# Hybrid mLSTM and DeltaNet layer step: the end of the kernel reordered, and the DeltaNet level product on 128x128 tiles

## The chip, the cores and the metric

One Trainium2 chip, one of its cores, one launch. The metric is the time of an execution on the device in microseconds (us); the number that counts is the median of the runs.

## The reference

One decoder layer for a prompt of 512 tokens and 8 sample sequences of 4 tokens (32 sample tokens), width 2048, all in f32. The layer is: a modulation of the input by `silu(c) @ w_ada`, one input projection, four mLSTM heads and eight gated DeltaNet heads, an output projection with a layer norm, a SwiGLU feed-forward block of inner width 5632 with a second layer norm, and the updated states. Two places matter here. The DeltaNet step solves, for each head and chunk, a unit lower triangular system:

```
A = bet[..., :, None] * jnp.einsum('bhld,bhsd->bhls', kh, kh) * decay * strict
sol = lax.linalg.triangular_solve(eye + A, rhs, left_side=True, lower=True, unit_diagonal=True)
```

and the layer ends with the down projection and a layer norm over the 2048 columns of each token, `(xf - mu) * lax.rsqrt(var + LN_EPS) * g + b`:

```
ffn = (jax.nn.silu(gate) * up) @ w_down
x = layer_norm(DEEPNORM_ALPHA * x + (1 + gt2) * ffn, ln2_g, ln2_b)
```

## The kernel before, in words

The kernel is one program for all engines. Activations stand transposed in SBUF, features on the 128 partitions and 544 columns of tokens (512 of the prompt, then 32 of the samples). A weight product is done in three passes of a rounded f32 format: `split` (L147) makes a high part of a weight on ScalarE (a copy, L97) and the remainder on VectorE (a subtraction, L100); the activations were split in the same way. `split_w` (L151) does it for eight blocks of 128x128 at a time, with two buffers for each part. Weights come in on SP's queue into three buffers (`raw_tile`). Helpers record every ScalarE activation at L97, every `tensor_tensor` at L100 (VectorE, or GpSimd where the call names it) and every `scalar_tensor_tensor` at L103.

The order on each engine is not the order of the text. A planner puts the instructions into each engine's stream before the launch, by the order of the text as priority and by its own estimate of when operands and buffers are there. Each engine then works through its stream in order, waiting on semaphores.

**DeltaNet.** `gdn_solve` (L595) prepares one head: four chunks of 128 tokens on the free dimension. It builds the inverse `U` of the triangular matrix by doubling: seven levels n, block size b = 2^n. Level 0 is a mask and transposes. In each of the six others (L646 to L679) GpSimd masks the coupling blocks into `Al` (128 x 4 chunks x 64 columns), VectorE copies the even blocks of `U` into `Ue`, TensorE transposes `Ue` (L666, two transposes for the four chunks), and multiplies `Al` of each chunk with the odd blocks of `U` (L669): four f32 products with 64 stationary and 64 moving columns, of which two chunks go to the upper and two to the lower 64 partitions of the PSUM tile `ps`. ScalarE copies the result into the block diagonal tile `P1` in two copies (L97), VectorE copies the transposes into `Tm`; a second product (L677, two f32 products of 128x128 with 128 columns) and a subtraction from the odd blocks of `U` end the level. `gdn_chain` (L682) then runs the recurrence over chunks. `weave` (L189, L1201) interleaves the solve of head hd+1 and the chain of head hd with the generator `fill` of dense projection products (L160), which keep TensorE supplied.

**The end.** `down` (L1502) is the down projection, in three rounds over the 44 blocks of the inner width (0 to 14, 14 to 28, 28 to 44). The last round has m = 0 to 11 over all 544 columns; m = 12 to 15 are done in two halves of the columns: first 0 to 256 (token tiles 0 and 1), then 256 to 544 (token tiles 2, 3 and the samples). A block m of a half is two loads of eight 128x128 weight blocks, 48 products (L1520) and an update of `z[m]` on VectorE (L103), with three small operations for the sample columns when the half has them. The half blocks and the turned tiles share a pool of three PSUM buffers (L1500).

`turned(j, ts)` (L1563) turns four feature blocks of each token tile with four transposes (L1569) into one PSUM tile, takes its statistics (L1570) and copies it to SBUF on ScalarE. The samples are the fifth token tile, with 32 of 128 partitions in use. `norm(t0, t1)` (L1573) aggregates the statistics, makes the reciprocal root by Ln and Exp on ScalarE for all its tiles together, and then goes through the tiles in four pieces of 512 columns: for the first three pieces Identity with scale and bias on ScalarE, the product with the gain on VectorE, the sum with the shift on GpSimd; for the fourth two fused operations on VectorE. Two stores of 1024 columns for each tile (L1595).

The order of the end (L1599 to L1611): m = 0 to 11, where after each four of them five tiles are turned; the first half of m = 12 to 15; of the second half m = 12; turning of tiles 0 and 1; m = 13; then m = 14 and 15 together with `norm(0, 2)`; turning of tiles 2, 3 and the samples; `norm(2, 5)`.

## Time and profile before

| | us |
|---|---|
| median of three runs (lowest to highest) | 3022.82 (3014.93 to 3023.85) |
| the profiled execution | 3026.12 |
| its span, first to last instruction | 3024.3 |
| TensorE busy in the span | 2934.8 |
| VectorE busy | 1710.0 |
| ScalarE busy | 1118.2 |
| GpSimd busy | 311.4 |

Engines in rows: PE is TensorE's matmul, PEld its weight load, DVE is VectorE, ACT ScalarE, POOL GpSimd, SP the engine that issues DMAs; a q behind the name marks the issuing side. A transpose stands as MATMUL too. Matmuls are pipelined: a record's duration is its way through the array, and what TensorE spends on it is the distance from its start to the next start. A row of the timeline merges instructions of one kind that follow each other (x8), with the start of the first, the time to the end of the last, and in brackets the idle time of the engine ahead of it and what ended that. Rows by window give for each stretch its length, busy time and number of instructions of each engine, the granted clock as a share of full speed, the busy share of the DMA engines and GB/s.

### The profile page before, as it was taken

How to read it: one execution, taken by the hardware profiler on the slowest of the kernel's cores; microseconds unless marked ns; L12 is line 12 of the kernel's file. 1: busy time of each engine (PE TensorE's matmuls, PEld its weight loads, DVE VectorE, ACT ScalarE, POOL GpSimd, SP SyncE). 2: the span in 40 equal slices, each digit the busy share in tenths (PEclk: the TensorE clock that was granted, in tenths of full speed). 3: DMA queues.
4: the chain of work that ended last, by engine and by line, in shares of the span. 5: the costliest groups of instructions: out<-in, count | busy, mean ns of one | idle time of the engine just before them, and what ended most of it. 6: DMA issues, size and time to landing. Idle time of an engine off the chain costs nothing.

```text
span 3024.3 us, 55954 instructions
## 1 busy us (share of the span) xinstructions
PE 2934.8 (97%) x22642; PEld 2733.7 (90%) x22642; DVE 1710.0 (57%) x3000; ACT 1118.2 (37%) x2053; POOL 311.4 (10%) x475
## 2 busy tenths in 40 slices
PE   8999999999999999999899999999999999999995
PEld 5788788888888989899799999999999999999995
DVE  2443433254555666655787777777777753333336
ACT  3333223234444444432354444444444432222224
POOL 0000101010121222210220000000000020000003
PEclk9999999999999999999899999999999999999998
DMA  8856666665445332443333433334343464433224
GB/s 271 283 161 171 200 189 192 196 200 165 148 124 157 90 89 68 132 131 102 121 111 114 118 113 109 113 113 120 106 116 113 117 214 112 138 105 110 84 78 135
DMA packets 567222, 418.02 MB, mean 138 GB/s; under 512 B 26956, under 2 KB 500132, under 8 KB 566964
## 3 DMA queue, kind: packets, MB, share of 16 engines
q1 hardware_dynamic: 554644, 378.74, 42.6%
q0 software_dynamic: 12320, 35.71, 3.4%
q8 instruction: 178, 2.92, 0.4%
q14 instruction: 80, 0.66, 0.1%
HBM read 374.21 MB, written 40.15 MB: 137 GB/s over the span
## 4 chain that ended last, share of the span: by engine, by line
PE 66%; issue 5%; DMA 2%; DVE 2%; ACT 2%; POOL 1%; SPq 0%; POOLq 0%; ACTq 0%; DVEq 0%
PE P L1380 29%; PE d L1520 16%; PE d L160 12%; PE P L1445 2%; PE m L1520 1%; PE a L232 1%; PE m L677 1%; DMA S<-in_state_gdn_S_dram 1%; PE m L669 1%; DMA raw<-in_w_out_dram 0%; ACT jk L97 0%; DVE lo L100 0%; ACT hi L97 0%; PE m L666 0%; PE m L807 0%
## 5 line engine op out<-in xcount | busy, mean ns | idle before, releaser
L97 ACT ACTIVATE hi<-raw 128x1024 fp32r<-128x1024 f32 (+3 forms) x384 | 369.0, 961 | 784.0 <-PE d L160 307.4
L100 DVE TENSOR_TENSOR lo<-raw,hi 128x1024 fp32r<-128x1024 f32 (+3 forms) x384 | 427.6, 1114 | 305.3 <-ACT hi L97 294.5
L160 PE MATMUL d<-hhi,hi 128*128 128x272 f32 x2048 | 461.2, 306 | 1.2 <-ACT hi L97 1.2
L160 PE MATMUL d<-hhi,lo 128*128 128x272 f32 x2048 | 429.4, 290 | 0.0
L160 PE MATMUL d<-hlo,hi 128*128 128x272 f32 x2048 | 427.7, 289 | 0.0
L160 PEld LDWEIGHTS d<-hhi,hi 128*128 128x128 f32 x2048 | 321.3, 189 | 86.3 <-issue 39.3
L160 PEld LDWEIGHTS d<-hlo,hi 128*128 128x128 f32 x2048 | 322.3, 189 | 3.2 <-issue 2.3
L160 PEld LDWEIGHTS d<-hhi,lo 128*128 128x128 f32 x2048 | 322.8, 189 | 0.9 <-issue 0.3
L100 DVE TENSOR_TENSOR lo<-lw,hi 128x1024 fp32r<-128x1024 f32 x84 | 103.0, 1226 | 181.7 <-ACT hi L97 181.7
L97 ACT ACTIVATE hi<-lw 128x1024 fp32r<-128x1024 f32 x84 | 89.2, 1062 | 193.6 <-PE P L1380 191.4
L1520 PE MATMUL d<-alo,hi 128*128 128x272 f32 x896 | 150.8, 290 | 4.1 <-DVE s L100 4.1
L103 DVE SCALAR_TENSOR_TENSOR s<-d,adaT,s 128x512 f32<-128x512 f32 x76 | 57.0, 750 | 171.2 <-PE d L1520 119.9
L1520 PE MATMUL d<-ahi,hi 128*128 128x272 f32 x896 | 149.3, 288 | 0.0
L1380 PE MATMUL P<-ahi,s 128*128 128x272 f32 x1008 | 140.5, 288 | 0.0
L1380 PE MATMUL P<-alo,s 128*128 128x272 f32 x1008 | 140.5, 288 | 0.0
L97 ACT ACTIVATE s<-lw 128x512 fp32r<-128x512 f32 x168 | 106.2, 632 | 84.8 <-PE P L1380 54.5
L1406 POOL DMA_DIRECT2D hid<-s x88 | 47.2, 543 | 828.1 <-DVE s L100 786.1
L1380 PEld LDWEIGHTS P<-ahi,s 128*128 128x128 f32 x1008 | 132.3, 188 | 0.0
L1380 PEld LDWEIGHTS P<-alo,s 128*128 128x128 f32 x1008 | 132.1, 188 | 0.1
L1520 PEld LDWEIGHTS d<-alo,hi 128*128 128x128 f32 x896 | 128.2, 190 | 4.3 <-issue 4.3
L1380 PE MATMUL P<-ahi,hi 128*128 128x272 f32 x672 | 130.0, 288 | 0.0
L1380 PE MATMUL P<-alo,hi 128*128 128x272 f32 x672 | 129.4, 287 | 0.0
(715 smaller groups left out, 6561.9 us busy)
## 6 DMA issues: line engine op xcount, KB each, us to landing
araw<-in_w_ada_dram SPq DMA_DIRECT2D x288, 256.0 KB, 3.9
raw<-in_w_in_dram SPq DMA_DIRECT2D x104, 512.0 KB, 5.5
raw<-in_w_gu_dram SPq DMA_DIRECT2D x168, 256.0 KB, 4.1
s<-in_w_gu_dram SPq DMA_DIRECT2D x168, 256.0 KB, 3.2
raw<-in_w_down_dram SPq DMA_DIRECT2D x72, 512.0 KB, 4.0
araw<-in_w_ada_dram SPq DMA_DIRECT2D x48, 512.0 KB, 6.0
raw<-in_w_out_dram SPq DMA_DIRECT2D x32, 512.0 KB, 4.8
raw<-in_w_down_dram SPq DMA_DIRECT2D x32, 384.0 KB, 3.5
```

The costliest lines, as they stand in the source:

```text
L97: A.activation(out, in_, func, **kw)
L100: eng.tensor_tensor(out, in0, in1, op)
L103: V.scalar_tensor_tensor(out, in0, scalar, in1, op0, op1)
L160: PE.matmul(ps[:, 240 + HALF * h:240 + HALF * (h + 1)], w_, a_[:, HALF * h:HALF * (h + 1)], start=f, stop=l)
L232: PE.matmul(ps[32 * g:32 * g + 32, :128 * nt], cT[:, q + g, :], rw[g // n][:, g % n, :], start=(q == 0), stop=end)
L669: PE.matmul(ps[r:r + 64, 64 * (c // 2):64 * (c // 2) + 64].rearrange("p (n b) -> p n b", b=b), Al[:, c, :], part(U, 1)[:, c], start=True, ...
L677: PE.matmul(ps[:, 256 + 128 * c:384 + 128 * c], ch(Tm, c), P1[:, c, :], start=True, stop=True)
L1380: PE.matmul(ps[n], w_[:, kk, :], block(b, x, k), start=f_, stop=l_)
L1406: G.dma_start(hid[2 * c + m][:, HALF * h:HALF * h + HALF], ut[m ^ h][:, HALF * m:HALF * m + HALF])
L1445: PE.matmul(acc_n[t][h], wn[m // 4 * 4, t // 2][:, m % 4, 128 * (t % 2):128 * (t % 2) + 128], z[m][:, HALF * h:HALF * h + HALF], start=(m ...
L1520: PE.matmul(ps[:, b - c0:e - c0], w_[:, kk, :], H[k][x][:, b:e], start=f, stop=l)
```

## The change

**DeltaNet (`gdn_solve`).** `Al` becomes one flat tile of 4 x 64 columns. Two chunks at a time are the stationary side of one product, 128 columns, and the odd blocks of the same two chunks its 128 moving columns. The result is 128x128 for a pair of chunks; the two 64x64 blocks on its diagonal are the wanted products, and the two copies into `P1` pick those. Two f32 products take the place of four.

**The end.** The samples leave `turned`: the new `norm_s` brings their 32 tokens x 2048 columns onto 128 partitions (four groups of 32 partitions, one for each 512 columns) with 16 products against the identity, takes statistics for each partition, combines the four groups with two products against `same4` (0.25 where two partitions belong to the same token), and normalises all in one 128x512 piece with gains and shifts that eight more loads put on the same partitions. The halves of m = 12 to 15 change places: columns 256 to 544 come first, 0 to 256 last, so that token tiles 0 and 1 are the last ones. Each block of a half has a yield between its two weight loads. The fourth turned part of tiles 0 and 1 stays in PSUM (`held`) and is normalised from there. The reciprocal root is Sqrt on ScalarE and a reciprocal on VectorE, with one Sqrt at the start of the stretch instead of the named table. All sums with the shift are on VectorE; the fourth piece is handled like the others. Stores of the last two tiles are 512 columns each.

```diff
@@ -645,7 +645,8 @@
         idb = ident.unsqueeze(1).to_broadcast([128, 4, 128])
         for n in range(7):
             b = 1 << n
-            Al = T(mp, [128, 4, 128], "Al", bufs=1)[:, :, :128 if n == 0 else 64]
+            al_ = T(mp, [128, 512], "Al", bufs=1)[:, :512 if n == 0 else 256]
+            Al = al_.rearrange("p (c t) -> p c t", c=4)
             part = lambda t, e: t.rearrange("p c (n e b) -> p c n e b", e=2, b=b)[:, :, :, e, :]
             if n == 0:
                 tt(Al, Am, lev[:, 0:1, :].to_broadcast([128, 4, 128]), ALU.mult, G)
@@ -664,18 +665,19 @@
             ps, pt = pst(), pst()
             for c in range(2):
                 PE.transpose(ch(pt, c), Ue[:, 2 * c:2 * c + 2, :].rearrange("p c t -> p (c t)"), ident)
-            for c in range(4):
-                r = 64 * (c % 2)
-                PE.matmul(ps[r:r + 64, 64 * (c // 2):64 * (c // 2) + 64].rearrange("p (n b) -> p n b", b=b),
-                          Al[:, c, :], part(U, 1)[:, c], start=True, stop=True)
-            for r in (0, 64):
-                act(P1[r:r + 64, :, r:r + 64], ps[r:r + 64, 0:128].rearrange("p (c s) -> p c s", c=2), AF.Copy)
+            uo = U.rearrange("p c (n e b) -> p (c n) e b", e=2, b=b)[:, :, 1, :]
+            for c in range(2):
+                PE.matmul(ch(ps, c).rearrange("p (n b) -> p n b", b=b), ch(al_, c),
+                          uo[:, 128 // b * c:128 // b * (c + 1)], start=True, stop=True)
+            for e in range(2):
+                r = 64 * e
+                act(P1[r:r + 64, :, r:r + 64],
+                    ps[r:r + 64, 0:256].rearrange("p (c e s) -> p c e s", c=2, e=2)[:, :, e, :], AF.Copy)
             Tm = T(mp, [128, 256], "Tm", bufs=1)
             V.tensor_copy(Tm, pt[:, 0:256])
             yield
             for c in range(2):
                 PE.matmul(ps[:, 256 + 128 * c:384 + 128 * c], ch(Tm, c), P1[:, c, :], start=True, stop=True)
-            uo = U.rearrange("p c (n e b) -> p (c n) e b", e=2, b=b)[:, :, 1, :]
             tt(uo, uo, ps[:, 256:].rearrange("p (n b) -> p n b", b=b), ALU.subtract)
             yield
 
@@ -1512,6 +1515,8 @@
             ahead.clear()
             for i, rw in enumerate(loaded):
                 n = min(8, k1 - k0 - 8 * i)
+                if i and c1 - c0 < NT:
+                    yield
                 h3, l3 = split_w(rw, n)
                 for k in range(k0 + 8 * i, k0 + 8 * i + n):
                     kk = k - k0 - 8 * i
@@ -1549,66 +1554,111 @@
 
 
     free = [t[:, :1024] for h in range(2) for t in cx_tiles(h, F32)]
-    yn, grow = [free[2 * t:2 * t + 2] for t in range(5)], free[10:12]
+    yn, grow, cx_last = [free[2 * t:2 * t + 2] for t in range(4)], free[8:10], free[10:12]
     brow = [T(lx, [128, 2 * NT], "lw%d" % i)[:, :1024] for i in range(2)]
     for row, n in ((grow, "ln2_g"), (brow, "ln2_b")):
         for i in range(2):
             SP.dma_start(row[i], a[n][1024 * i:1024 * i + 1024].unsqueeze(0).to_broadcast([128, 1024]))
-    bst = T(lx, [128, 5, 4, 6], "bst")
-    mv = T(lx, [128, 5, 4], "mv")
-    V.memset(mv, 1.0)
-    A.preload_act_table_set("natural_log_exp_and_others")
-    rows = [128] * 4 + [NS]
+    bst = T(lx, [128, 4, 4, 6], "bst")
+    mv = T(lx, [128, 4, 4], "mv")
+    act(mv[:, 0, 0:1], eps_l, AF.Sqrt)
+
+    def turn_tile(j, t):
+
+        ps = pst()
+        for i in range(4):
+            PE.transpose(ps[:, 128 * i:128 * i + 128], z[4 * j + i][:, 128 * t:128 * t + 128], ident)
+        V.bn_stats(bst[:, t, j, :], ps)
+        return ps
+
+    def y_of(t, j):
+        return yn[t][j // 2][:, 512 * (j % 2):512 * (j % 2) + 512]
+
+    def row_of(x, j):
+        return x[j // 2][:, 512 * (j % 2):512 * (j % 2) + 512]
 
     def turned(j, ts):
-
         for t in ts:
-            n, c = rows[t], 512 * (j % 2)
-            ps = pst()
-            for i in range(4):
-                PE.transpose(ps[:n, 128 * i:128 * i + 128], z[4 * j + i][:, 128 * t:128 * t + n], ident)
-            V.bn_stats(bst[:n, t, j, :], ps[:n])
-            act(yn[t][j // 2][:n, c:c + 512], ps[:n], AF.Copy)
-
-    def norm(t0, t1):
-        for t in range(t0, t1):
-            V.bn_aggr(mv[:rows[t], t, 0:2], bst[:rows[t], t, :, :])
-        act(mv[:, t0:t1, 2], mv[:, t0:t1, 1], AF.Ln, bias=eps_l)
-        act(mv[:, t0:t1, 2], mv[:, t0:t1, 2], AF.Exp, scale=-0.5)
-        stt(mv[:, t0:t1, 3], mv[:, t0:t1, 0], -1.0, mv[:, t0:t1, 2], ALU.mult, ALU.mult)
-        for t in range(t0, t1):
-            n = rows[t]
-            mean, rstd, off = (mv[:n, t, i:i + 1] for i in (0, 2, 3))
+            act(y_of(t, j), turn_tile(j, t), AF.Copy)
+
+    def scales(m):
+
+        mean, var, rstd, off = (m[..., i:i + 1] for i in range(4))
+        act(rstd, var, AF.Sqrt, bias=eps_l)
+        V.reciprocal(rstd, rstd)
+        stt(off, mean, -1.0, rstd, ALU.mult, ALU.mult)
+
+    def norm(ts, held=None):
+
+        for t in ts:
+            V.bn_aggr(mv[:, t, 0:2], bst[:, t, :, :])
+        scales(mv[:, ts[0]:ts[-1] + 1])
+        for t in ts:
+            for j in (3, 0, 1, 2) if held else range(4):
+                y = y_of(t, j)
+                act(y, held[t] if held and j == 3 else y, AF.Identity, scale=mv[:, t, 2:3], bias=mv[:, t, 3:4])
+                tt(y, y, row_of(grow, j), ALU.mult)
+                tt(y, y, row_of(brow, j), ALU.add)
+                if held:
+                    SP.dma_start(y_p[0, 128 * t:128 * t + 128, 512 * j:512 * j + 512], y)
+                elif j % 2:
+                    SP.dma_start(y_p[0, 128 * t:128 * t + 128, 512 * j - 512:512 * j + 512], yn[t][j // 2])
+                yield
+
+    def norm_s():
+
+        ps = pst()
+        for i in range(4):
             for j in range(4):
-                c = slice(512 * (j % 2), 512 * (j % 2) + 512)
-                y, g_, b_ = (x[j // 2][:n, c] for x in (yn[t], grow, brow))
-                if j < 3:
-                    act(y, y, AF.Identity, scale=rstd, bias=off)
-                    tt(y, y, g_, ALU.mult)
-                    tt(y, y, b_, ALU.add, G)
-                else:
-                    stt(y, y, mean, g_, ALU.subtract, ALU.mult)
-                    stt(y, y, rstd, b_, ALU.mult, ALU.add)
-                if j % 2:
-                    c = slice(1024 * (j // 2), 1024 * (j // 2) + 1024)
-                    dst = y_p[0, 128 * t:128 * t + 128, c] if t < 4 else y_s2[:, c]
-                    SP.dma_start(dst, yn[t][j // 2][:n])
-            yield
+                PE.matmul(ps[32 * j:32 * j + 32, 128 * i:128 * i + 128], z[4 * j + i][:, SEQ:], ident, start=True,
+                          stop=True)
+        V.bn_stats(sst, ps)
+        act(ys, ps, AF.Copy)
+        V.bn_aggr(ms[:, 0:2], sst.unsqueeze(1))
+        yield
+
+        ps = pst()
+        PE.matmul(ps[:, 0:1], same4, ms[:, 0:1], start=True, stop=True)
+        tt(ms[:, 2:3], ms[:, 0:1], ps[:, 0:1], ALU.subtract)
+        V.tensor_copy(ms[:, 0:1], ps[:, 0:1])
+        stt(ms[:, 1:2], ms[:, 2:3], ms[:, 2:3], ms[:, 1:2], ALU.mult, ALU.add)
+        yield
+        PE.matmul(ps[:, 1:2], same4, ms[:, 1:2], start=True, stop=True)
+        V.tensor_copy(ms[:, 1:2], ps[:, 1:2])
+        scales(ms)
+        act(ys, ys, AF.Identity, scale=ms[:, 2:3], bias=ms[:, 3:4])
+        tt(ys, ys, gbs[:, 0], ALU.mult)
+        tt(ys, ys, gbs[:, 1], ALU.add)
+        for j in range(4):
+            SP.dma_start(y_s2[:, 512 * j:512 * j + 512], ys[32 * j:32 * j + 32])
+        yield
 
     y_s2 = y_s.rearrange("b t c -> (b t) c")
+
+    gbs = cx_last[0][:, :1024].rearrange("p (x c) -> p x c", x=2)
+    ys = cx_last[1][:, :512]
+    ms, sst = cx_last[1][:, 512:516], cx_last[1][:, 516:522]
+    same4 = cx_last[1][:, 528:656]
+    for x, n in enumerate(("ln2_g", "ln2_b")):
+        for j in range(4):
+            SP.dma_start(gbs[32 * j:32 * j + 32, x], a[n][512 * j:512 * j + 512].unsqueeze(0).to_broadcast([32, 512]))
+    V.tensor_reduce(same4[:, 0:32], ident.rearrange("p (j t) -> p t j", j=4), mybir.AxisListType.X, ALU.add)
+    V.tensor_scalar(same4[:, 0:32], same4[:, 0:32], 0.25, None, ALU.mult)
+    V.tensor_copy(same4[:, 32:128].rearrange("p (j t) -> p j t", j=3),
+                  same4[:, 0:32].unsqueeze(1).to_broadcast([128, 3, 32]))
     part = down(range(12), 28, 44)
     for j in range(3):
         for _ in range(4):
             next(part)
-        turned(j, range(5))
-    drain(down(range(12, 16), 28, 44, 0, 256))
-    part = down(range(12, 16), 28, 44, 256, NT)
+        turned(j, range(4))
+    drain(down(range(12, 16), 28, 44, 256, NT))
+    part = down(range(12, 16), 28, 44, 0, 256)
     next(part)
-    turned(3, range(2))
     next(part)
-    run_gens(part, norm(0, 2))
-    turned(3, range(2, 5))
-    drain(norm(2, 5))
+    turned(3, (2, 3))
+    run_gens(part, chain(norm_s(), norm((2, 3))))
+    held = {t: turn_tile(3, t) for t in (0, 1)}
+    drain(norm((0, 1), held))
     op_stack.close()
     lx_stack.close()
     pj_stack.close()
```

## Rows read from the trace of the kernel before

**Rows 1.** The page: TensorE's busy time, share of the span and instructions, and its busy tenths in 40 slices of the span.

```profile
PE 2934.8 (97%) x22642; PEld 2733.7 (90%) x22642; DVE 1710.0 (57%) x3000; ACT 1118.2 (37%) x2053; POOL 311.4 (10%) x475
PE   8999999999999999999899999999999999999995
```

**Rows 2.** Busy time by window, the DeltaNet stage.

```profile
775.00:1300.00 525.00, 508.71 (x4138) 461.99 (x4138) 320.65 (x740) 235.18 (x621) 119.50 (x183) 1.00 0.39 112
```

**Rows 3.** The instructions of L669: durations in ns (least, median, most), first and last start in us, form.

```profile
L669 PE MATMUL m<-s,Al x192: 218/222/275, 778.5 to 1214.4; 128*64 128x64 f32 x192
...
L669 PE MATMUL m<-U,Al x192: 218/222/273, 833.9 to 1296.6; 128*64 128x64 f32 x192
```

**Rows 4.** Timeline from the last weight product to the last store, rows of PE, DVE, ACT and SP.

```profile
2991.01 0.82 PE L1569 MATMUL m<-cst,s 128*128 128x128 f32 x6
...
2992.13 0.47 DVE L103 SCALAR_TENSOR_TENSOR s<-m,adaT,s 128x256 f32<-128x256 f32 x1
...
2993.30 0.68 DVE L1570 BATCH_NORM_STATS2 bst<-m 128x6 f32<-128x512 f32 x1
...
2995.73 0.48 DVE L1575 BATCH_NORM_AGGREGATE mv<-bst 128x2 f32<-128x24 f32 x3
...
2996.44 1.28 ACT L97 ACT_TABLE_LOAD   x1
2997.73 0.30 ACT L97 ACTIVATE mv<-mv,cst 128x3 f32<-128x3 f32 x1
2998.05 1.28 ACT L97 ACT_TABLE_LOAD   x1
...
2999.58 0.17 DVE L103 SCALAR_TENSOR_TENSOR mv<-mv 128x3 f32<-128x3 f32 x1 [2.10 <-ACT mv L97]
2999.79 1.52 ACT L97 ACTIVATE c4a<-c4a,mv 128x512 f32<-128x512 f32 x2 [0.23 <-DVE mv L103]
...
3017.37 0.32 SPq L1595 DMA_DIRECT2D out_dram<-c3b  x1
```

**Rows 5.** Timeline of the half-width part, rows of DVE and PE.

```profile
2953.50 0.48 DVE L103 SCALAR_TENSOR_TENSOR s<-m,adaT,s 128x256 f32<-128x256 f32 x1 [0.63 <-PE m L1520]
...
2959.15 0.48 DVE L103 SCALAR_TENSOR_TENSOR s<-m,adaT,s 128x256 f32<-128x256 f32 x1 [0.63 <-PE m L1520]
...
2970.97 1.03 PE L1569 MATMUL m<-cst,s 128*128 128x128 f32 x8
2971.17 0.48 DVE L103 SCALAR_TENSOR_TENSOR s<-m,adaT,s 128x256 f32<-128x256 f32 x1 [0.99 <-PE m L1520]
...
2979.78 1.22 DVE L100 TENSOR_TENSOR lo<-raw,hi 128x1024 fp32r<-128x1024 f32 x1
...
2981.01 1.28 DVE L100 TENSOR_TENSOR c0a<-c0a,c4b 128x512 f32<-128x512 f32 x2
...
2990.39 1.82 DVE L103 SCALAR_TENSOR_TENSOR c3a<-c3a,mv,lw 128x512 f32<-128x512 f32 x1
```

**Rows 6.** Timeline of PE in the DeltaNet stage: one level, and two products of the chain.

```profile
996.31 0.38 PE L666 MATMUL m<-cst,Ue 128*128 128x128 f32 x2
996.62 0.45 PE L669 MATMUL m<-U,Al 128*64 128x64 f32 x8
997.00 0.52 PE L160 MATMUL d<-hhi,hi 128*128 128x272 f32 x2
997.36 0.42 PE L160 MATMUL d<-hlo,hi 128*128 128x272 f32 x2
...
999.37 0.61 PE L677 MATMUL m<-P,Tm 128*128 128x128 f32 x4
999.73 0.50 PE L160 MATMUL d<-hhi,hi 128*128 128x272 f32 x2
1000.07 0.41 PE L160 MATMUL d<-hlo,hi 128*128 128x272 f32 x2
...
1093.22 0.38 PE L689 MATMUL m<-S,s 128*128 128x128 f32 x2
1093.44 0.39 PE L690 MATMUL m<-S,s 128*128 128x128 f32 x2
```

**Rows 7.** Timeline of PE in the full-width part: one turning of the samples.

```profile
2838.57 0.60 PE L1569 MATMUL m<-cst,s 128*32 128x128 f32 x4
2838.92 0.50 PE L1520 MATMUL d<-alo,hi 128*128 128x272 f32 x2
```

**Rows 8.** Timeline at the step from the full-width to the half-width part, rows of ACT and PE.

```profile
2938.40 0.60 ACT L97 ACTIVATE c1a<-m 128x512 f32<-128x512 f32 x1 [2.00 <-DVE bst L1570]
2939.05 1.31 PE L1569 MATMUL m<-cst,s 128*128 128x128 f32 x8 [1.93 <-ACT c1a L97]
```

**Rows 9.** Busy time by window in the half-width part (PE, PEld, DVE, ACT, POOL, then the granted clock).

```profile
2940.40:2943.80 3.40, 3.40 (x16) 3.40 (x17) 0.69 (x2) 1.18 (x2) 0.00 (x0) 0.51 0.15 45
...
2971.00:2991.00 20.00, 20.00 (x153) 19.91 (x152) 18.59 (x32) 13.68 (x17) 9.22 (x4) 1.00 0.35 106
```

**Rows 10.** Timeline of PE in the DeltaNet stage: a product that waits for another engine.

```profile
1091.22 1.09 PE L807 MATMUL m<-S,kq 128*64 128x128 f32 x8 [1.15 <-POOL kq L100]
```

**Rows 11.** Timeline of SP's queue at the step from the second to the third round of the down projection.

```profile
2784.00 0.57 SPq L1556 DMA_DIRECT2D c4b<-in_ln_g_dram  x1
...
2789.38 5.14 SPq L144 DMA_DIRECT2D raw<-in_w_down_dram  x2
```

More of the change, by code (lines that the diff above doesn't have):

```diff
@@ L2 @@
 from contextlib import ExitStack
-from itertools import islice, zip_longest
+from itertools import chain, islice, zip_longest
 import numpy as np
```

## The prediction

> **What bounds the kernel now.** I read the page first: the busy shares and the slices. TensorE is busy 97% of the span, nine tenths or more in nearly every slice, and only the last slice falls to five tenths [rows 1]. So what is taken off TensorE's stream counts nearly in full until its last weight product, and behind that product something else sets the end. Each part of the change has its own stretch, and is priced there.
>
> In the DeltaNet stage (775 to 1300 us) TensorE is busy 508.7 of 525 us, VectorE 320.7, ScalarE 235.2, GpSimd 119.5 [rows 2]: TensorE is the bound and the others only time its rare stops. The level product stands in the trace as 2 x 192 = 384 records on 128*64 tiles [rows 3], that is 8 heads x 6 levels x 4 chunks x 2 records for an f32 product: 48 groups of eight.
>
> The end I read in the timeline, backwards. The last weight product is over at 2991.01, where the turning of the last tiles begins; the last store is issued at 3017.37 [rows 4]; the span ends at 3024.3. From the last product to the end are 33.3 us in which TensorE hardly works. In them VectorE and GpSimd work side by side in SBUF and slow each other: an operation on 128x512 takes 0.64 us where VectorE is alone (two in 1.28) and 1.82 beside GpSimd [rows 5]. Two table loads of 1.28 us stand between the statistics and the first normalised value [rows 4].
>
> **The change part by part.**
>
> **DeltaNet product: -6.2 us.** Before, two transposes start at 996.31, the eight half-width records at 996.62, the next dense pair at 997.00 and the pair behind it at 997.36 [rows 6]: 1.05 us. In this the two transposes hold 0.31 us, where two full records followed by full ones hold 0.22 (1093.22 to 1093.44); entering the half-width shape costs time outside the group. After, the group is four full 128x128 f32 records, the very shape of the second product of the same level: 999.37 to 999.73, then a dense pair to 1000.07, together 0.70 [rows 6]. With 0.22 for the transposes that is 0.92, so 0.13 less, 48 times: -6.2. Bounds: if only the group itself counts, 0.38 against 0.36, it is -1.0. If the four records take 0.11 each like those at 1093, 0.44 against 0.38 and no gain outside, it is +2.9. I take -6.2, since every shape in the sum has a row and the stage is TensorE's. The two evictions, the transposed copy and GpSimd's mask keep count and size: nothing. The first eviction now waits for the last record rather than an earlier one; the dense products between the two halves of a level hide that.
>
> The Trainium skill, page "TensorEngine Tiling (Array Packing)", section "Theoretical Speedup", promises up to twice the speed to a product whose stationary side has at most 64 columns; by that the merged product would cost up to twice the 0.38 us, which is a rival below. The same page's "Key Properties" says that a change of tiling mode drains the engine, and the 0.31 against 0.22 of rows 6 agrees with it.
>
> **Turning of the samples: 0.** Three turnings of the 32-token tile leave TensorE's stream in the full-width part; one holds 0.35 us (2838.57 to 2838.92) [rows 7], -1.0 in all. norm_s puts 16 f32 products (32 records) on 128*32 tiles instead, four column groups at once: as an estimate eight steps at the 0.11 of a 128-column record plus entry and exit, +1.1.
>
> **The step into the half-width part: -0.6.** Five turned tiles pass three PSUM buffers there, and TensorE waits 1.93 us at 2939.05 for the first copy [rows 8]. With four tiles, one copy (0.6) less has to be over before the next product. The clock's fall to 0.51 right behind [rows 9] I leave as it is, since a wait of the same kind stays.
>
> **Waits that are added: +1.0.** Three products of norm_s hang on small VectorE and ScalarE work. TensorE takes its stream in order, so the weight products behind them wait too, and behind those the copies that free the weight tiles. The nearest rows are 1.93 us (a turning that waits for a copy) and 1.15 us (a product that waits for GpSimd's mask) [rows 8, 10]. Two waits at half the smaller: +1.0; bounds 0 and +4. The eight added loads of gains pass SP's queue ahead of weight loads: at 0.57 us of issue each 4.6 us, where the next weight load came 5.4 us after the first gain load [rows 11]; weights are three tiles ahead, so nothing, and without that cover up to 4.6 once.
>
> **The end: -8.0.** Let S be the turning of tiles 2 and 3. From S to the last product TensorE has three output blocks of 256 columns at 5.65 us (from update to update, 2953.50 to 2959.15), 1.0 for the turning [rows 5] and 1.1 for the samples: 19.1 us. In this time VectorE is given five weight remainders at 1.22 (6.1), three updates at 0.48 (1.4), three statistics at 0.68 (2.0) [rows 4, 5], their aggregates (0.6), nine small steps of the samples at 0.17 (1.5), two rows of the samples (1.3) and eight pieces of 128x512 at 1.28 for tiles 2 and 3 (10.2): 23.1 us. In the same stretch VectorE is now busy 18.6 of 20 us [rows 9], so 1.4 idle; 17.7 get done and 5.4 are left over at the last product. What follows, by rows of the present end [rows 4]: 0.2 to the update (as 2970.97 to 2971.17), 1.2 from the update to the first statistics, 1.3 for two of them, 0.4 aggregates, 0.35 root, 0.2 reciprocal (no row has it at this size; between 0.17, a small step, and 0.68, a full-width one, nearer the first), 0.2 offset, 0.8 for the first Identity: 4.7 us, of which 2.3 leave VectorE free for the leftover. Then sixteen operations at 0.64 (10.2), the other 3.1 of the leftover, and from the last store's issue to the end 7.0 as now plus 0.3, the last store being larger: 25.3 against 33.3. Gone are the sample tile's four pieces, both table loads (2.6) and every 1.82. Bounds: no leftover at all, -11.1; all of it behind and another 0.7 lost, -5.
>
> That the root keeps one table for good rests on the rows so far only by likeness: Identity follows the second load without another [rows 4]. The Trainium skill, page "ScalarE: Activation LUTs", section "Table sets: the hidden batching unit", says that one set holds both Ln and Exp, so that one load serves both; by that only 1.3 us would go here. The trace shows two loads in a row, and the rows decide.
>
> **Sum.** -6.2 + 0 - 0.6 + 1.0 - 8.0 = -13.8 us. The profiled execution took 3026.12 us, 1.8 over its span and 3.3 over the median of the runs; from the median, 3022.8 - 13.8 = 3009.0.
>
> **Rivals.**
> 1. *The merged product gives nothing*, because TensorE's gain turns into waits for the level's copies. For it: ScalarE's evictions and VectorE's subtraction time every level. Against it: TensorE stands still for only 16 of 525 us [rows 2]. Time: 3009.0 + 6.2 = about 3015. Chance 0.13.
> 2. *VectorE becomes the bound of the end*: the order on each engine is planned beforehand, the leftover stays in front of the last tiles, and the weights' remainders come late too. For it: VectorE is full already [rows 9] and takes over GpSimd's additions. The end then gains 4 rather than 8 and the waits cost 2 more: about 3015. Chance 0.15.
> 3. *Slower: the samples' products stop TensorE long enough for its clock to fall.* At 2939.05 it had stood 1.93 us, and soon after it ran at 0.51, the lower of its levels (1.2 instead of 2.4 GHz) [rows 8, 9]. If each of the three products waits for VectorE's leftover (some 3 us each, +9) and the 17 us of blocks behind them run at half clock (+17), the sum is +12: about 3035. It decides once the waits pass some 3 us each with the clock down. Against it: in that stretch TensorE is now busy 20 of 20 us beside a full VectorE. Chance 0.07.
> 4. *Slower: half-width tiles are worth their factor of two.* Then the merged product costs 0.38 more, 48 times, +18 instead of -6: about 3033. Against it: the same shape at 0.36 [rows 6]. Chance 0.03. This is the rule of the tiling page.
>
> **How the numbers follow.** Forecast 0.62, rivals 0.13, 0.15, 0.07 and 0.03. 0.3%, about what a measurement can tell from no change, is 9.1 us, so the line lies at 3013.7. The forecast's own bounds are 3005 (no wait, no leftover: -6.2 - 0.6 - 11.1) and 3020 (-1.0 - 0.6 + 4 - 5); the runs shown lie 9 us apart, so the lower end goes to 3001, and rivals 1 and 2 are inside. Range 3001 to 3019. Rivals 1 and 2 lie near the line, mostly above it: faster 0.66, same 0.24, slower 0.10.
>
> **What would show it.** Right: the level product as four records on 128*128 tiles (192 in all), about 0.92 us from the first transpose to the second dense pair; no GpSimd work behind the last product; VectorE's pieces at 0.64; no table load at the end; some 25 us from the last product to the end. Wrong: over 4 us of idle time before the samples' products, a granted clock under 1 between S and the last product, more than four leftover pieces behind the last product, or waits in the DeltaNet stage that grow by the 6 us saved.

## The result and the profile after

| | before | after |
|---|---|---|
| median of six runs, taken side by side | 3021.55 us | 3004.06 us |
| lowest to highest | 3014.93 to 3024.44 | 3003.07 to 3006.33 |
| ratio, 95% interval | | 0.9949 [0.9940, 0.9959] |
| the profiled execution, its span | 3026.12, 3024.3 | 3004.57, 3002.8 |

By the ratio the change takes off 15.4 us (12 to 18); 13.8 were forecast. The profiled spans lie 21.6 us apart, and stretches that the change does not touch make up the difference: the DeltaNet stage begins at 760.8 before and 757.8 after, and over all thirteen traces of this study that start varies from 754.1 to 760.8. Below, stretches are compared, not spans, and products are counted from their starts. Five of them carry the result (from the timelines); they add up to some 15.5 us:

| us | before | after |
|---|---|---|
| first solve to last inverse level of the DeltaNet stage | 537.3 | 533.6 |
| first weight product of the down projection to its last full-width one | 490.1 | 488.4 |
| last full-width product to last product | 55.6 | 58.1 |
| last product to the end of the span | 33.5 | 19.3 |
| TensorE's wait at the layer norm behind the output projection | 7.0 | 8.6 |

The page of the kernel after, parts 1 and 2, beside [rows 1]: TensorE's last slice rises from five tenths to seven, GpSimd loses 15 operations.

```profile
PE 2927.0 (97%) x22470; PEld 2738.0 (91%) x22470; DVE 1702.9 (57%) x3016; ACT 1114.4 (37%) x2050; POOL 282.7 (9%) x460
PE   8999999999999999999899999999999999999997
```

The instructions of the merged product, L670, of the kernel after (columns as in [rows 3]): 192 records on 128*128 where there were 384 on 128*64.

```profile
L670 PE MATMUL m<-s,Al x96: 273/275/280, 774.9 to 1206.6; 128*128 128x128 f32 x96
...
L670 PE MATMUL m<-U,Al x96: 273/275/347, 830.6 to 1290.0; 128*128 128x128 f32 x96
```

One level in TensorE's timeline, after, beside [rows 6]: transposes at 991.33, product at 991.55 (0.22 later, not 0.31), second dense pair at 992.25. The level takes 0.92 us, the number of the forecast.

```profile
991.33 0.38 PE L667 MATMUL m<-cst,Ue 128*128 128x128 f32 x2
991.55 0.61 PE L670 MATMUL m<-U,Al 128*128 128x128 f32 x4
991.91 0.49 PE L160 MATMUL d<-hhi,hi 128*128 128x272 f32 x2
992.25 0.41 PE L160 MATMUL d<-hlo,hi 128*128 128x272 f32 x2
```

The end in the timeline, after, beside [rows 4]. The last weight product starts at 2983.50. VectorE still owes four pieces of token tile 3 (c1b; the last tiles, 0 and 1, stand in c0a to c3a), but they mostly fill the pauses of the chain update, statistics, aggregates, root, reciprocal. The first piece of the last two tiles starts at 2989.24, sixteen operations follow at 0.6 each, and the last store goes out at 2999.23, 3.6 us before the end. There is no table load in this stretch, and no GpSimd.

```profile
2983.82 0.48 DVE L103 SCALAR_TENSOR_TENSOR s<-m,adaT,s 128x256 f32<-128x256 f32 x1
2984.22 0.68 DVE L100 TENSOR_TENSOR c1b<-c1b,lw 128x512 f32<-128x512 f32 x1
...
2985.42 0.69 DVE L1571 BATCH_NORM_STATS2 bst<-m 128x6 f32<-128x512 f32 x1
...
2987.23 0.38 DVE L1594 BATCH_NORM_AGGREGATE mv<-bst 128x2 f32<-128x24 f32 x2
2987.64 0.30 ACT L97 ACTIVATE mv<-mv,cst 128x2 f32<-128x2 f32 x1 [9.12 <-DVE mv L1594]
2987.97 0.17 DVE L1588 RECIPROCAL mv<-mv 128x2 f32<-128x2 f32 x1 [0.36 <-ACT mv L97]
...
2989.24 0.69 DVE L100 TENSOR_TENSOR c1a<-c1a,c3b 128x512 f32<-128x512 f32 x1 [0.91 <-ACT c1a L97]
...
2998.51 0.69 DVE L100 TENSOR_TENSOR c3a<-c3a,lw 128x512 f32<-128x512 f32 x1
2999.23 0.33 SPq L1603 DMA_DIRECT2D out_dram<-c3a  x1
```

Busy time from the turning of tiles 2 and 3 to the last product, after, beside [rows 9]: TensorE 20.4 of 21 us at a granted clock of 1.00, VectorE 19.0.

```profile
2962.60:2983.60 21.00, 20.40 (x196) 19.80 (x194) 19.01 (x37) 14.87 (x20) 0.00 (x0) 1.00 0.44 139
```

### The profile page after: what moved, and what is told of

Its sections match the earlier page's. It is cut to its first block, busy times and chain, and to the rows that moved or that the text cites. A ratio compares the mean times of both kernels' runs of the same rounds, so it can differ in the third digit from the quotient of the medians.

```text
span 3002.8 us, 55607 instructions
## 1 busy us (share of the span) xinstructions
PE 2927.0 (97%) x22470; PEld 2738.0 (91%) x22470; DVE 1702.9 (57%) x3016; ACT 1114.4 (37%) x2050; POOL 282.7 (9%) x460
## 4 chain that ended last, share of the span: by engine, by line
PE 67%; issue 5%; DVE 3%; DMA 2%; ACT 2%; POOL 0%; SPq 0%; ACTq 0%; DVEq 0%; POOLq 0%
PE P L1382 29%; PE d L1525 16%; PE d L160 12%; PE P L1447 2%; PE m L1525 1%; PE a L232 1%; PE m L680 1%; PE m L670 1%; PE m L809 0%; DVE lo L100 0%; PE m L667 0%; ACT jk L97 0%; DVE y L103 0%; DMA raw<-in_w_out_dram 0%; DMA out_dram<-hn 0%
## 5 line engine op out<-in xcount | busy, mean ns | idle before, releaser
L97 ACT ACTIVATE hi<-lw 128x1024 fp32r<-128x1024 f32 x84 | 89.1, 1060 | 194.0 <-PE P L1382 191.8
L232 PE MATMUL a<-araw,cT 128*32 128x512 f32 (+1 forms) x832 | 124.9, 582 | 2.7 <-DMA araw<-in_w_ada_dram 2.1
```

Source lines behind the costliest of these rows:

```text
L97: A.activation(out, in_, func, **kw)
L232: PE.matmul(ps[32 * g:32 * g + 32, :128 * nt], cT[:, q + g, :], rw[g // n][:, g % n, :], start=(q == 0), stop=end)
```

## The experiments

Differences "to before" come from the ratio to runs of the kernel before on the same chip; the others are differences of these.

**Each part alone.** `gdn_only` is the kernel before with the merged product; `end_only` is the kernel after with the old product:

```
-  for c in range(4):                      # the four half-width products of a level
-      PE.matmul(ps[r:r + 64, ...], Al[:, c, :], part(U, 1)[:, c], ...)
+  for c in range(2):                      # gdn_only has these, end_only the four
+      PE.matmul(ch(ps, c)..., ch(al_, c), uo[:, ...], ...)
```

> The kernel before with the DeltaNet product alone changed. Theory (TensorE is the bound there, the change of shape was the cost): a level takes 0.92 us from the first transpose to the second dense pair instead of 1.05, 48 levels give 6.2, of which some comes back as waits: total -3 to -6 us, the end of the kernel as before (33 us from the last weight product to the end). Rival (the gain turns into waits for the level's copies): 0 within 1.5. Rival (half-width tiles are worth a factor of two): +18.

> The changed kernel with the old DeltaNet product. Theory: the end alone gives -11 to -13 us (the profile after has 19.2 us from the last weight product to the end against 33.3, less a last product that comes 2.4 later counted from the step into the half-width part), and the two parts add up to the whole. Rival (the parts share a gain, as by the phase of the clock): the sum of this and of the DeltaNet product alone misses the whole by over 4 us.

`gdn_only`: 0.9986 [0.9978, 0.9995], -4.2 us, inside what was expected. `end_only`: 0.9965 [0.9952, 0.9977], -10.6, a little under the 11 to 13 expected. Together -14.8 of the whole's -15.4: within the intervals the parts add up, and over two thirds of the change is its end.

**What a half-width tile is worth.** `four_full` is the kernel after with four products of 64 moving columns per level on the full stationary tile:

```
-  for c in range(2): PE.matmul(ch(ps, c)..., ch(al_, c), uo[:, 128 // b * c:128 // b * (c + 1)], ...)
+  for c in range(4): PE.matmul(ps[:, 64 * c:64 * c + 64]..., ch(al_, c // 2), uo[:, 64 // b * c:64 // b * (c + 1)], ...)
```

> The kernel after, but each level's first product in four products of 64 moving columns with the 128x128 stationary tile, where it now has two products of 128 columns: same columns, same full-width tiles, twice the products. Theory (what the half-width tiles cost is the change of the tile's shape, not the number of products): 0.92 to 1.0 us per level, against 1.05 of before; total 0 to +3 us over the kernel after. Rival (the number of products and weight loads costs): 1.05 to 1.15 us per level, +5 to +9 us over the kernel after, all that the merging gained.

1.0016 [1.0005, 1.0026] to before, +20 us over the kernel after: the theory fell, and so far that even its rival was too mild. One level of `four_full` in TensorE's timeline:

```profile
989.39 0.38 PE L667 MATMUL m<-cst,Ue 128*128 128x128 f32 x2
989.61 1.00 PE L670 MATMUL m<-U,Al 128*128 128x64 f32 x8
990.42 0.50 PE L160 MATMUL d<-hhi,hi 128*128 128x272 f32 x2
990.76 0.41 PE L160 MATMUL d<-hlo,hi 128*128 128x272 f32 x2
```

Eight records on the full stationary tile hold TensorE for 0.81 us (989.61 to 990.42), 0.10 each, though they move only 64 columns; the merged four, with 128 columns, 0.36, or 0.09 each; the old eight on half-width tiles 0.38, or 0.05 each [rows 6]. The single records of the three traces (medians over the 48 levels) say more. Full-width ones start 0.11 us apart, with 64 moving columns as with 128: at this size the columns moved make no difference. Half-width ones start in pairs, the two 0.01 us apart, with the first pair 0.11 and each later one 0.06 us ahead of the next. What takes this gain back lies around the group: the first half-width record starts 0.20 us after the second transpose (0.11 at full width), and the next dense product 0.15 us after the last (0.03). The Trainium skill, page "TensorEngine Tiling (Array Packing)", section "Theoretical Speedup", gives a narrow stationary side up to twice the speed. For the whole group, 0.38 against 0.81, that agrees; inside it a pair in 0.06 against one record in 0.11 is more. The merge wins all the same, because it does the work with half the records, at the same price for the group, and saves the entry into the other shape.

**What the end gains from.** `nopool_before` is the kernel before with a single edit, and `pool_sum` the kernel after with the reverse one; `swap_only` is the kernel before with the order of the last stretch alone:

```
nopool_before  - tt(y, y, b_, ALU.add, G)               + tt(y, y, b_, ALU.add)
pool_sum       - tt(y, y, row_of(brow, j), ALU.add)     + tt(y, y, row_of(brow, j), ALU.add, G)
swap_only      - drain(down(..., 0, 256)); part = down(..., 256, NT); ...; run_gens(part, norm(0, 2)); ...; drain(norm(2, 5))
               + drain(down(..., 256, NT)); part = down(..., 0, 256); ...; run_gens(part, norm(2, 5)); ...; drain(norm(0, 2))
```

> The kernel before, with one edit: the sums of the second layer norm go from GpSimd to VectorE; order of the end, samples on 32 partitions, Ln and Exp, and the DeltaNet inverse stay. Theory (what the end gained is mostly the loss of GpSimd: VectorE's 1.7 to 1.75 us per operation beside it go back to 0.65, and GpSimd's closing drain no longer holds the end): from the scales at 8.6 us after the last product there are 22 operations of VectorE left at 0.65 = 14.3 us, then 0.3 + 3.6 us to the end: tail 26 to 28 us for 33.5, total -5.5 to -8 us, ratio 0.9973 to 0.9982. Rival (the order of the end and the samples on 128 partitions carry the gain, and VectorE pays for the sums what the sharing cost it): tail 32 to 34, total -1.5 to +1 us.

> The changed kernel with the sum with the shift of every prompt piece on GpSimd again (the samples' piece stays on VectorE). Theory (GpSimd beside VectorE slows both): VectorE's products of the last tiles take 1.74 instead of 0.68 us as soon as GpSimd has work, the weights' remainders stretch too, the last store is issued 4 to 7 us later; and the 7 us from the last store's issue to the end come back instead of 3.6, since GpSimd's closing drain ran from 3014.59 to 3023.56 in the kernel before and had nothing to do in the changed one: +7 to +11 in all. Rival (the sums simply move off VectorE, eight pieces of 0.61 each way): -3 to +1.

> The kernel before with the halves of blocks 12 to 15 exchanged and nothing else: tiles 2, 3 and the samples first and normalised beside the last blocks, tiles 0 and 1 last; Ln and Exp, GpSimd's sums and the sample tile on 32 partitions stay. Theory (most of the end's gain is two tiles instead of three behind the last product, each tile some 6.7 us of paired VectorE and GpSimd work): -3 to -7 us. Rival (GpSimd beside VectorE is the cost, and the third tile's work only comes earlier and stops TensorE): -2 to +3.

`nopool_before`: 0.9971 [0.9960, 0.9983], -8.7 us, more than expected: 23.8 us from the last product to the end, for 33.5. `pool_sum`: 1.0003 [0.9994, 1.0012]; the whole gain is gone, some 16 us where 7 to 11 were expected. The stretch from the last full-width product to the end is 3.0 us longer than before, which takes up most of DeltaNet's part as well. `swap_only`: 1.0005 [0.9996, 1.0014], so its rival came true; it shortens the end to 26.3 us and lengthens the half-width part by 8.1: three tiles now meet the weights' remainders on VectorE beside GpSimd, TensorE waits 4.8 us for them, and from the end of the longer of two waits (4.2) the granted clock is 0.50 up to the last product, 5 us. The end of `pool_sum`, timeline of VectorE and GpSimd:

```profile
2997.27 0.69 DVE L100 TENSOR_TENSOR c1a<-c1a,c3b 128x512 f32<-128x512 f32 x1 [0.91 <-ACT c1a L97]
2997.97 2.36 DVE L100 TENSOR_TENSOR c0a<-c0a,c2b 128x512 f32<-128x512 f32 x2
2998.04 1.75 POOL L100 TENSOR_TENSOR c1a<-c1a,lw 128x512 f32<-128x512 f32 x1 [10.24 <-DVE c1a L100]
...
3000.26 1.75 DVE L100 TENSOR_TENSOR c1a<-c1a,c3b 128x512 f32<-128x512 f32 x1
...
3001.93 1.75 DVE L100 TENSOR_TENSOR c3a<-c3a,c3b 128x512 f32<-128x512 f32 x1
```

Here a piece of VectorE takes 0.69 us at 2997.27, alone, and 1.75 at 3000.26, beside GpSimd. One operation of each engine takes 1.67 us (3000.26 to 3001.93), and VectorE alone does both kinds in 0.6 each, 1.2 together: here the second engine is no help but a loss. In the end of `nopool_before` no piece takes 1.75, and the samples' pieces on 32 partitions (c2b, two in 1.27 us) cost what full ones cost:

```profile
3000.60 0.68 DVE L100 TENSOR_TENSOR c1b<-c1b,lw 128x512 f32<-128x512 f32 x1
...
3001.20 1.27 DVE L100 TENSOR_TENSOR c2b<-c2b,c4b 32x512 f32<-32x512 f32 x2
```

From the last full-width product to the end of the span before took 89.1 us, `nopool_before` 78.4, `end_only` 77.1. So of the 12.0 us that the end gives, 10.7 come from the sums that left GpSimd (4.0 of them behind the last store's issue, 7.0 to 3.0), and 1.3 from all the rest: order, samples, root. That is one order of taking the steps. In the other, `pool_sum` takes 92.0 us in this stretch and the kernel after 77.4: the sums are then worth 14.7, and the rest, with GpSimd still at work (16 sums for 15), costs 3.0.

**What the rest does.** `samples_32` is the kernel after with the samples as a fifth tile of 32 partitions, turned in every round and normalised with tiles 2 and 3, without norm_s; `ln_exp` has the old root:

```
samples_32  - turned(j, range(4)); turned(3, (2, 3)); run_gens(part, chain(norm_s(), norm((2, 3))))
            + turned(j, range(5)); turned(3, (2, 3, 4)); run_gens(part, norm((2, 3, 4)))
ln_exp      - act(rstd, var, AF.Sqrt, bias=eps_l); V.reciprocal(rstd, rstd)
            + act(rstd, var, AF.Ln, bias=eps_l); act(rstd, rstd, AF.Exp, scale=-0.5)
```

> The changed kernel with the samples as a fifth token tile on 32 partitions, turned with the others and normalised with tiles 2 and 3 beside the last blocks; order of the halves, root, VectorE's sums and the held pieces stay. Theory (an operation costs its columns, not its partitions: four pieces of 1.22 us instead of one, less the samples' small steps of some 1.5): 2 to 3 us more for VectorE in a stretch where it is full, +2 to +3. Rival (the two products with same4 and their small steps cost TensorE as much as they save): within 1.

> The changed kernel with the reciprocal root by Ln and Exp again, with the named table set ahead. Theory (two loads of 1.28 us on the path behind the last statistics, a reciprocal of 0.17 less): the first normalised piece of the last tiles 2.6 us later, the end +2.3; beside it four more loads in the half-width part, which ScalarE hides or which stop TensorE for under 1. Rival (VectorE's leftover fills the wait and the end is VectorE's sum): under +1.

`samples_32`: 0.9970 [0.9959, 0.9981], some 6 us over the kernel after, twice what was expected: the step into the half-width part back at 5.4 us (4.5 after, 5.1 before), the full-width part of the down projection back at 490.2, and the end 3.1 longer. `ln_exp`: 0.9958 [0.9943, 0.9973], 2.7 over the kernel after, but the interval holds the kernel after. Its trace has the end 3.1 longer and 2.0 more up to the last product, where TensorE waits 2.1 us for a weight copy on ScalarE, which has four loads in that part; 1.6 us come back elsewhere (see "The table" below). In the traces each is worth more beside the others than the 1.3 above. Then the order of the halves alone, with the old samples and the old root, should cost time; `swap_only` points that way beside GpSimd's sums, and without them no run tried it.

**Why the end follows the last store sooner.** `pool_last` is the kernel after with one tiny GpSimd copy behind the last piece:

```
+ G.tensor_copy(cx_last[1][:, 660:661], y_of(1, 2)[:, 511:512])
```

> The changed kernel with one GpSimd copy of a 128x1 column behind the last normalised piece, which nothing waits for. Theory (GpSimd's drain takes some 6 us from its last operation and ends after SP's): the last store's issue stays, the end comes 6.5 to 7 instead of 3.6 us after it, +3 to +4. Rival (the 7 us of the kernel before belonged to its stores or to GpSimd's long operations): within 0.5 of the changed kernel.

0.9954 [0.9937, 0.9970]: the interval holds the kernel after, so the verdict is the profile's: 23.05 us from the last product to the end, +3.8, all of it behind the last store. Its last store and copy in the timeline (span 3005.9):

```profile
2998.62 0.33 SPq L1603 DMA_DIRECT2D out_dram<-c3a  x1
2998.75 0.19 POOL L1662 COPY c5b<-c3a 128x1 f32<-128x1 f32 x1 [539.89 <-DVE c3a L100]
```

The closing line of the program, GpSimd's queue, in `pool_last`, before and after (durations in ns; first and last start in us):

```profile
L1693 POOLq DRAIN  x3: 46/102/6417, 2998.7 to 3005.7; - x3
```

```profile
L1642 POOLq DRAIN  x3: 46/102/8963, 3014.6 to 3024.1; - x3
```

```profile
L1692 POOLq DRAIN  x3: 46/102/7542, 2457.6 to 3002.5; - x3
```

Before, GpSimd's drain is issued at 3014.6 and lasts 8.96 us, to 3023.6, 6.2 behind its last operation (3015.64 + 1.70) and 0.8 ahead of the end. In `pool_last` it runs from 2998.7 to 3005.2, 6.2 behind a copy of 0.19 us. After, the long drain begins at 2457.6 and is over long before the end. In all thirteen traces this drain ends 6.2 us behind GpSimd's last operation. So it held the end: 7.0 us from the last store's issue before, 3.6 after, 7.3 in `pool_last`.

**A faster end.** `early_turn` is the kernel after without its last two `next(part)`, so that tiles 2 and 3 are turned one output block sooner. `early_stt` adds to this that VectorE does the first piece of the last two tiles alone, its first half while ScalarE takes the root:

```
early_turn  - next(part); next(part)
early_stt   + stt(y_of(t, 3), held[t], mv[:, t, 0:1], row_of(grow, 3), ALU.subtract, ALU.mult)   # beside the root
            + stt(y, y, mv[:, t, 2:3], row_of(brow, j), ALU.mult, ALU.add)                       # behind the reciprocal
```

> The changed kernel, but tiles 2 and 3 are turned right behind the first half, before block 12 of the second half, so that their normalising has one block more of TensorE time beside it. Theory (VectorE's leftover stands in front of the last tiles: five pieces of 0.68 us and the weights' remainder that TensorE waits 0.6 us for): the leftover goes, -3 to -4.5 us against the changed kernel, the end 16 us from the last product. Rival (the order on VectorE is set by the weights and the statistics, the pieces come no sooner): within 1 us of the changed kernel.

> early_turn, and in the last two tiles the first piece is done by VectorE alone: (y - mean) * gain while ScalarE takes the root, then * rstd + bias behind the reciprocal, so that VectorE does not wait for root and ScalarE's first piece. In early_turn VectorE's idle times there are 0.37 and 0.90 us and the same number of its operations follows. Theory (the tail is VectorE's chain): tail 16.7 to 17.3 us for 18.15, total 1 to 1.5 us under early_turn, ratio to the kernel before 0.9933 to 0.994. Rival (the operations with two scalars cost more and the stores or ScalarE set the end): tail 18 or more, ratio 0.994 to 0.9946.

`early_turn`: 0.9941 [0.9927, 0.9954], 2.4 us under the kernel after, less than expected, and the interval holds the kernel after, so again the trace decides; last full-width product to end 74.9 us for 77.4. `early_stt`: 0.9938 [0.9925, 0.9950], median 3000.74 us, 73.7; its end is 16.9 us for 18.15, as expected (the 0.9 between their times is within the intervals). It has the lowest median here. VectorE no longer stops between the aggregates and the pieces:

```profile
2985.18 0.38 DVE L1594 BATCH_NORM_AGGREGATE mv<-bst 128x2 f32<-128x24 f32 x2
2985.48 0.73 DVE L103 SCALAR_TENSOR_TENSOR c1a<-m,mv,c3b 128x512 f32<-128x512 f32 x1
2985.60 0.30 ACT L97 ACTIVATE mv<-mv,cst 128x2 f32<-128x2 f32 x1 [7.40 <-DVE mv L1594]
2986.13 0.74 DVE L103 SCALAR_TENSOR_TENSOR c3a<-m,mv,c3b 128x512 f32<-128x512 f32 x1
2986.79 0.15 DVE L1599 RECIPROCAL mv<-mv 128x2 f32<-128x2 f32 x1
```

## Why the prediction held, step by step

The forecast was 3009.0 us, -13.8; measured were 3004.06 and -15.4. Sign and place of the two large terms were right, their sizes were not: DeltaNet gave 2.0 to 2.5 us less than forecast, the end 6 more. The half-width part cost 1 us more than its terms, and a cost of 1.6 at another layer norm stood in no term. That the total came within 1.6 us is in part luck, since these errors cancel.

**DeltaNet product, -6.2: right per level, and a third was lost elsewhere.** Summed over the 48 levels in TensorE's timeline, first transpose to second dense pair, they took 49.1 us before and 44.2 after: -4.9. One of the levels after, at 1280.02, takes 2.02 us, since the dense product behind it waits 0.62 for ScalarE and the clock then falls to 0.50; at the usual 0.92 the sum would be -6.0, close to the forecast. That level is no accident of one trace: it takes 1.45 to 2.02 us in all eight with the merged product, and in the four with the old one no level takes over 1.14. `gdn_only` gained 4.2, and the stage got 3.7 shorter; over the traces it takes 537.1 to 539.8 us with the old product (four) and 532.4 to 536.1 with the merged one (eight), 3.8 apart in the mean. The step that failed is that every other wait of the stage stays as it is. TensorE's waits from 1190 to 1300 us (in total, times, longest), before, and then after:

```profile
PE m L561 <- DVE exs L103: 2.5, 1, 2.5
```

```profile
PE m L561 <- DVE exs L103: 3.4, 1, 3.4
```

and the busy time behind that wait, after:

```profile
1220.20:1227.00 6.80, 5.68 (x27) 5.68 (x27) 4.14 (x15) 2.54 (x10) 0.00 (x0) 0.50 0.28 82
```

The wait is 2.5 us in the four traces with the old product (before, `nopool_before`, `swap_only`, `end_only`) and 3.4 to 3.8 in the eight with the merged one (in `four_full`, whose levels take 1.37 us, it is 2.5 too); around its end the granted clock is 0.50, the lower of its two levels (1.2 GHz), for 3.4 to 6.8 us in each of these eight, and for 3.4 in one of the four. By estimate 3.4 us at half clock cost 1.7, so waits and clock are enough for what is missing. That they are its whole cause is not shown: no run took this wait away, and why exs does not come sooner with the rest stays open.

**Turning of the samples, 0: right within 0.5.** The full-width part of the down projection takes 487.6 to 488.8 us in the traces with four tiles and 489.0 to 490.3 in those with five: the -1.0, or a little more. The samples' sixteen products take 1.08 us instead, and the two with `same4` 0.25:

```profile
2966.42 1.08 PE L1613 MATMUL m<-cst,s 128*32 128x128 f32 x32
```

**Step into the half-width part, -0.6: right in size, not in reason**, 5.09 to 4.49 us, and 5.40 again in `samples_32`. The forecast had one copy less to wait for; TensorE's wait is the same, 1.93 before [rows 8] and 1.94 after, and what is gone are the samples' four transposes behind it:

```profile
2929.20 0.66 PE L1570 MATMUL m<-cst,s 128*128 128x128 f32 x4 [1.94 <-ACT c1a L97]
```

**Added waits, +1.0: 0.6, at another place.** The waits of norm_s never stop TensorE (each of its small products holds it 0.13 us). One wait is there, for a weights' remainder that is late behind VectorE's pieces:

```profile
2980.94 0.38 PE L1525 MATMUL m<-alo,lo 128*128 128x256 f32 x1 [0.60 <-DVE lo L100]
```

With the samples' products (1.08 and 0.25) and six transposes of tiles 0 and 1, which now stand ahead of the last product (0.55), this makes 2.5 of the 3.1 us by which the half-width part grew, its step not counted. The eight gain loads took 4.1 us of SP's queue for the 4.6 worked out, and TensorE did not wait for them:

```profile
2775.07 1.97 SPq L1644 DMA_DIRECT2D c4b<-in_ln_g_dram  x4
2777.08 2.15 SPq L1644 DMA_DIRECT2D c4b<-in_ln_b_dram  x4
```

**The end, -8.0: too small.** It was to take 25.3 us and took 19.3. The term of the sixteen operations was right (10.2, measured 10.0 from 2989.24 to 2999.23). The leftover of VectorE was sized at 5.4 us, 3.1 of them in the way; it was four pieces, and most went into pauses of the chain: 5.7 us to the first piece, where 7.8 was worked out. And "from the last store's issue to the end 7.0 as now plus 0.3" was the wrong step: it is 3.6, because the 7.0 were GpSimd's drain and not the store. The two make 5.8 of the 6.0 us. The reason given for the gain, that VectorE's and GpSimd's operations slow each other, is what `nopool_before` and `pool_sum` bear out.

**The table.** No load stands at the end, but the reason was not the one given. The early root does not stand at the start of this stretch: it was put at 1377.78, a load ahead of it, and its table was gone again by 1476.93. The load for the last norm stands at 2965.18, beside TensorE's work. ScalarE in the kernel after:

```profile
1377.78 0.20 ACT L97 ACTIVATE mv<-cst 128x1 f32<-128x1 f32 x1
...
1476.93 1.28 ACT L97 ACT_TABLE_LOAD   x1
1478.23 0.75 ACT L97 ACTIVATE lw<-lw,cst 128x544 f32<-128x544 f32 x1
1478.99 1.28 ACT L97 ACT_TABLE_LOAD   x1
...
2965.18 1.28 ACT L97 ACT_TABLE_LOAD   x1
```

The two loads at 1477 stand in front of Ln and Exp of the layer norm behind the output projection (L1252, L1253), which the change does not touch. In the kernel before the same Ln and Exp follow each other without a load:

```profile
1485.23 0.75 ACT L97 ACTIVATE lw<-lw,cst 128x544 f32<-128x544 f32 x1 [1.77 <-DVE lw L103]
1486.02 0.66 ACT L97 ACTIVATE lw<-lw 128x544 f32<-128x544 f32 x1
```

TensorE waits behind this norm, before and then after:

```profile
1491.39 4.00 PE L1445 MATMUL P<-s,c0b 128*128 128x272 f32 x8 [7.03 <-ACT s L97]
```

```profile
1485.37 4.12 PE L1447 MATMUL P<-s,c0b 128*128 128x272 f32 x8 [8.60 <-ACT s L97]
```

The wait is 7.0 us in the five traces without the early root and 8.3 to 8.6 in the eight with it. So the early root costs 1.3 to 1.6 us, a term that the prediction lacks, and `ln_exp`, which has no early root, gets it back. In the last stretch of `ln_exp` each Ln and each Exp stands behind a load of its own; the first two of six:

```profile
2961.67 1.28 ACT L97 ACT_TABLE_LOAD   x1
...
2965.41 1.28 ACT L97 ACT_TABLE_LOAD   x1
```

The prediction weighed the rule of the Trainium skill, page "ScalarE: Activation LUTs", section "Table sets: the hidden batching unit", that one set serves both Ln and Exp. The traces show both sides of it. Before, with the named set asked for at the start of the program, no load stands between 0.74 and 1549.16 us, and Ln and Exp run on one table there; behind a load for another function, each of the two got its own load. For the end the rows were the right guide; that one table can't hold both would be the wrong lesson.

**The rivals.** 1 (the merge gives nothing): no, though a third of it went where this rival looked, into waits. 2 (VectorE the bound of the end): its mechanism is there, not its time. From 2973.7 on the chain that ended last runs over VectorE almost without a break, and `early_stt`, `ln_exp` and `samples_32` move the end by what they take off it or put on it; but without GpSimd its pieces are short enough. 3 (clock): no, 1.00 in the window above; TensorE did not wait for the samples' products. 4 (half-width tiles worth a factor of two): `four_full` shows the factor; the merge halves the records, so it cancels.

## What to carry to other kernels

Where VectorE and GpSimd share a stretch that sets the end, price both alone first: moving GpSimd's part to VectorE gave 8.7 us with one edit, more than the reordering around it. Read the last microseconds of a span by engine: what closes last, a store or a drain, decides whether a shorter chain shows. Merging small products pays by records and by shapes left out, while waits further on in the same stage can take a share. And look where the planner put a small operation that changes ScalarE's table: the early root cost a layer norm that stands 1500 us ahead of the one it was written for.

## What the hardware showed

- GpSimd's closing drain ends 6.2 us after its last operation (all thirteen traces; in `pool_last` after a copy of 0.19 us).
- VectorE's piece of 128x512 takes 0.6 us alone and 1.75 beside a GpSimd operation, on 32 partitions as on 128 (before, from 3009.48: two on 32 partitions in 3.40). One of each takes 1.67 us.
- f32 records on a full stationary tile start 0.11 us apart, with 64 moving columns as with 128. On half-width tiles they start in pairs, a pair every 0.06 us, and such a group is entered 0.09 us later and left 0.12 us later than a full-width one.
- Ln and Exp run on one table where the named set is in force (before, 1485.23 and 1486.02) and take a load of 1.28 us each where another function was loaded in between (after, 1476.93 and 1478.99).
